# A four-layer conditioned network on one core: the steps of the conditioning are dealt out differently over its phases

## The chip, the core and the metric

The kernel runs on one core of a Trainium2 chip. Time is device time of the whole program in microseconds (us); lower is better. The engines that matter here are PE (matrix products; its weight loads are listed as PEld), DVE (elementwise work), ACT (activations), POOL (elementwise work) and SP, which here only issues transfers, one after the other. PE's clock has two levels, 1.2 and 2.4 GHz; the profile's granted clock (PEclk) is 1.00 where it ran at 2.4 GHz all the time.

## The reference, cut to what matters

Two blocks of two layers each run over 256 latent tokens and 256 context tokens of width 1024. Every layer has a mixer (gated linear attention, state space, two kinds of attention) and a feed-forward part (in the last layer, a mixture of experts). Everything is float32. Each layer's shifts, scales and gates are a product of one vector with a [1024, 6144] matrix: the **conditioning**, which is what the change moves about.

```
def first_block(x, c, ctx, c_ctx, ada_w, ada_b, ...):
    hl, hc = x, ctx
    s_lat = jax.nn.silu(c)
    s_ctx = jax.nn.silu(c_ctx)
    for i in range(DEPTH):
        m_l = jnp.split((s_lat @ ada_w[i] + ada_b[i])[:, None, :], 6, axis=-1)
        m_c = jnp.split(s_ctx @ ada_w[i] + ada_b[i], 6, axis=-1)
        ul = snake(modulate(hl, m_l[0], m_l[1]))
        uc = modulate(hc, m_c[0], m_c[1])
        ...
        hl = layer_norm(DEEPNORM_ALPHA * hl + m_l[2] * snake(yl), ln_g[i, 0], ln_b[i, 0])
        hl = layer_norm(DEEPNORM_ALPHA * hl + m_l[5] * sq_relu_mlp(modulate(hl, m_l[3], m_l[4]), ffn_w1[i], ffn_w2[i]),
                        ln_g[i, 1], ln_b[i, 1])
```

The second block has the same pattern with other norms and mixers.

## The kernel before, in words

The phases follow each other: mixer 0 (gated linear attention), feed-forward 0, mixer 1 (state space), feed-forward 1 (256 tokens only, where feed-forward 0 has 512), mixer 2 (attention), feed-forward 2 (gated, 512 tokens), mixer 3, experts. A product of float32 operands is made of three matmuls of split operands (`mm3`, L441 to L443). A unit of weights (`load`, L421) is 512 KB: SP fetches it into one of four buffers `wraw` (L431), ACT writes its upper bits to `whi` (L419), DVE the rest to `wlo` (L420). `whi` and `wlo` have four buffers each, so the loads run ahead of PE until these are full.

The conditioning (`ada`, L527) is a generator of 192 steps: 4 layers times 6 parts times 8 steps. A step fetches 512 KB of `ada_w`, and is done in one of two ways. **On PE** (L541): four products of 256 columns into the four row groups of one bank (8 records in the profile), from a buffer `araw` of a small pool of its own. **On DVE** (`on_pe` false, L559 and L562): the 512 KB go into one of the four `wraw` buffers, and DVE multiplies by the vector and adds to a sum `aacc`, once for the latents and, where the context needs the part, once more for the context; after a part's eighth step PE sums over the partitions ("pick", four products per sum). A part ends with four small DVE operations (L568 to L574); parts 2 and 5, the gates, are also written to memory, and `gates` (L624) reads them back as rows on all partitions.

Who takes steps, and when: `weave` (L591) alternates a mixer's main part with filler products, and after each main step adds a number of conditioning steps on PE (second number of `PACE`); `spread_ada` (L607) does steps on DVE after each step of a feed-forward product (`FPACE`); `project` takes one on PE per unit of weights. None goes beyond `CAPS`, which are per phase. The framework then orders each engine's instructions by when they should be ready, so that the rows on an engine are near the order of the code but not in it.

```
    def spread_ada(self, gen, a):
        for _ in gen:
            self.carry += a
            while self.carry >= 1:
                self.carry -= 1
                self.on_pe = False
                self.fill(1)
                self.on_pe = True
```

Of the kernel before, what the change touches and what calls it, by code (L numbers as in the profile page):

```python
# [13 lines left out]
PSUM = bass.MemoryType.PSUM  # L14
# [8 lines left out]
# ---------------------------------------------------------------- host layout  # L23
# [11 lines left out]
def _ws(w, n=256):  # L35
    """[K, C] -> [C/n, 128, K/128 * n]: all of K for n columns."""
    k, c = w.shape
    return _f(w.reshape(k // 128, 128, c // n, n).transpose(2, 1, 0, 3).reshape(c // n, 128, (k // 128) * n))


def _xs(w, kk=4, n=512):
    """[K, C] -> [K/(128 kk), C/n, 128, kk * n]."""
    k, c = w.shape
    return _f(w.reshape(k // (128 * kk), kk, 128, c // n, n).transpose(0, 3, 2, 1, 4)
              .reshape(k // (128 * kk), c // n, 128, kk * n))


def _xs_pad(w):
    """[K, C] with K no multiple of 512 -> [ceil(K/512), C/512, 128, 2048], k-tiles of the last unit shared out evenly."""
# [17 lines left out]
def _ev_bias(rpb):  # L67
    """Relative position bias by query and key, with the column window's -1e30: [8, 128, 2 * 256]."""
# [22 lines left out]
def _col(v):  # L91
    """[n * 128] -> [128, n]."""
    return np.asarray(v).reshape(-1, 128).T


def _ada_tiles(L, c):
    """The feature tiles of the conditioning's group c; the first layer's shift and scale come in halves."""
# [39 lines left out]
def layout(inp):  # L137
    """The arrays the program takes; every one a rearrangement of an input or a constant."""
    A = {}
# [19 lines left out]
    # GLA  # L159
# [19 lines left out]
    # SSD  # L179
# [9 lines left out]
    # second block  # L189
# [55 lines left out]
    # constants of the shapes  # L245
# [24 lines left out]
# ---------------------------------------------------------------- the program  # L270
# [11 lines left out]
# steps of filler, and of the conditioning, per step of a phase's main part  # L282
PACE = (0.7, 0.3), (0.45, 0.6), (1.3, 0.3), (1.3, 0.6), (0.9, 0.5), (0.65, 0.5), (0.25, 0.3), (1.25, 0.5), (0.26, 0.3)
# the conditioning's steps per step of the feed-forward layers, and how far it goes in each phase
FPACE = 0.35, 0, 0.25
CAPS = 72, 144, 144, 144, 144, 999, 999
# PSUM banks of the last mixer
OB = 2, 3, 1, 2
NREST = 2
# how many instructions a piece of work goes before its place, or after it  # L290
# [22 lines left out]
class Net:  # L313
# [4 lines left out]
    # ------------------------------------------------ pools, constants  # L318
    def pool(self, name, bufs=1, **k):
        """A pool and what closes it."""  # L320
# [3 lines left out]
    def banks(self, mm, tp, at=0, sc=0):  # L324
        """PSUM of a phase: accumulators, transposes, and two kinds for the mixers."""
# [62 lines left out]
    def open_h(self, es):  # L388
        """The residual, tokens on partitions: two tiles of the context, two of the latents."""
# [26 lines left out]
    # ------------------------------------------------ products of split operands  # L416
    def split(self, hi, lo, t, eng=None):
        """hi: the upper bits of t; lo: the exact rest."""
# [3 lines left out]
    def load(self, ap, n):  # L422
        """A unit of weights, split, in two halves: w(o, n) = parts of the columns o .. o + n."""
# [14 lines left out]
    def mm3(self, ps, a, b, first, last):  # L438
        """ps += a.T @ b."""
# [5 lines left out]
    def ws_acc(self, w, nm, m, x, t0, nt, ps):  # L445
        """Yields every 3072 columns or so."""
# [5 lines left out]
    def gemm_ws(self, ap, x, evac, nm=2, span=None):  # L452
        """Weights stationary: a unit of nm * 128 columns, tokens moving; evac(m, psum [columns, tokens])."""
# [8 lines left out]
    def gemm_ws_halves(self, units, x):  # L462
        """Several units at once, the context's tokens first: units = [(ap, nm, evac)]."""
# [14 lines left out]
    def gemm_xs(self, units, x, tts, n, evac, fill=0):  # L478
        """Tokens stationary: units = [(ap, ks)], each n columns of the weights of the k-tiles ks."""
# [22 lines left out]
    def unit(self, w, ks, x, pss, first, last, evac=None):  # L502
        """Part of a product with tokens stationary: pss = {token tile: psum}; w(k) the weights of k-tile k, split."""
# [8 lines left out]
    def flush(self):  # L512
        """What was put off until the tensor engine has other work behind it."""
# [10 lines left out]
    # ------------------------------------------------ conditioning  # L524
    def ada(self):
        """Every layer's conditioning vectors, in small steps."""
# [64 lines left out]
    def weave(self, main, filler, r, a=0.0):  # L591
        """After each step of main r steps of filler and a of the conditioning; then the rest of filler."""
        x = y = 0.0
        n = m = 0
        for _ in main:
# [6 lines left out]
            while y >= 1:  # L602
                y -= 1
                self.fill(1)
        k = sum(1 for _ in filler)

    def spread_ada(self, gen, a):  # L607
        """After each step of gen a of the conditioning, on the vector engine."""
# [8 lines left out]
    def need(self, L, c):  # L617
        """The conditioning's parts of layer L up to c."""
# [5 lines left out]
    def gates(self, pool, L, c, ctx=True):  # L624
        """Part c of the conditioning as rows on all partitions: {pair: [128, 1024]}."""
# [11 lines left out]
    def modvec(self, L, csh, csc, g=None, b=None):  # L637
        """Scale and shift per feature: (h*g + b) * (1 + scale) + shift."""
# [14 lines left out]
    # ------------------------------------------------ feature-major operands  # L653
    def big(self, i, h, dt=F32):
        """Half h of the 32 KB buffer i (per partition): [128, 4096]."""
# [9 lines left out]
    def fill_u(self, u, src, p, sc=None, sh=None):  # L665
        """Feature-major split copy of the token tiles src[0..1] of pair p, scaled and shifted."""
# [14 lines left out]
    def fill_u1(self, u, src, t, sc, sh):  # L681
        """The same of token tile t alone."""
# [12 lines left out]
    # ------------------------------------------------ norms  # L695
# [6 lines left out]
    def layernorm(self, t, c, pool, gb, bb, nz=3, z=None, keep=True, dump=None):  # L702
        """Called as each half c of H is there. z = (H - mean) * rstd, returned with the second half; later H = z * g + b."""
# [30 lines left out]
    def rms(self, t, c, pool, nz=4, z=None):  # L734
        """The same with H * rstd; c None: both halves at once."""
# [1563 lines left out]
```

## Time and profile before

| | |
|---|---|
| median of 3 runs (lowest, highest) | 2680.12 us (2672.77, 2683.09) |
| span of the profiled execution | 2672.4 us; the nearest run is 0.4 us above it |
| busy, share of the span | PE 94%, PEld 77%, DVE 73%, ACT 46%, POOL 25% |
| mean granted clock of PE | 0.974 |
| mixer 0 and its w_out | 0 to 418 us |
| feed-forward 0 | 418 to 795 us |
| mixer 1 and its w_out | 795 to 1212 us |
| feed-forward 1 | 1212 to 1405 us |
| mixer 2 and its w_out | 1405 to 1670 us |
| feed-forward 2 | 1670 to 2010 us |
| mixer 3, experts | 2010 to 2672 us |

PE's share is a mean over stages: some have PE at work without a gap, others have short waits of PE for DVE. What a moved step is worth is therefore read stage by stage.

### The profile page before, as it was taken

Reading aid. Unit: us, or ns where it says so; the run is one execution under the profiler, and the core shown is the slowest. Engines: PE = TensorE matmul, PEld = TensorE weight load, DVE = VectorE, ACT = ScalarE, POOL = GpSimd, SP = SyncE. Lnnn points to the kernel's source line nnn. Section 1 sums busy time; section 2 is a strip of 40 time slices with the busy share of each in tenths; the row PEclk is TensorE's granted clock in tenths of the full one; section 3 lists DMA queues with packets and bytes.
Section 4 is the critical chain, followed back from the end, with each engine's and each line's share of the span. In section 5 each row is a group of like instructions: output and inputs, shape, how many; then the busy total and the mean of one; then the engine's idle time right before and its main releaser. Section 6 shows DMA issues by size and latency. Waiting matters only on the chain.

```text
span 2672.4 us, 38317 instructions
## 1 busy us (share of the span) xinstructions
PE 2524.6 (94%) x14350; PEld 2065.7 (77%) x14350; DVE 1962.1 (73%) x3015; ACT 1239.3 (46%) x1899; POOL 659.3 (25%) x533
## 2 busy tenths in 40 slices
PE   6999999999999989899999999999999898999998
PEld 3877668877777777778988877888888676888886
DVE  3566787799988777877566457756438776999987
ACT  2433444223246555545544344322225444878775
POOL 1122334032332333424224123112124431000000
PEclk8999999999999989998999999999999998999999
DMA  8334556665642222245553225555524125999995
GB/s 283 125 129 142 195 200 205 213 219 198 209 161 94 71 67 71 71 159 173 189 188 122 78 71 174 180 194 194 191 92 163 61 72 193 341 328 356 336 334 217
DMA packets 137506, 471.66 MB, mean 176 GB/s; under 512 B 16544, under 2 KB 21792, under 8 KB 137056
## 3 DMA queue, kind: packets, MB, share of 16 engines
q1 hardware_dynamic: 131264, 458.34, 50.8%
q10 hardware_dynamic: 6048, 10.80, 1.2%
q8 instruction: 115, 1.88, 0.3%
q14 instruction: 79, 0.65, 0.1%
HBM read 467.96 MB, written 1.11 MB: 176 GB/s over the span
## 4 chain that ended last, share of the span: by engine, by line
PE 52%; DVE 8%; issue 4%; POOL 3%; ACT 2%; DMA 0%; ACTq 0%; DVEq 0%; POOLq 0%
PE b L441 15%; PE b L443 15%; PE b L442 15%; DVE wlo L420 2%; DVE FZ L1198 1%; PE b L1396 1%; POOL hrs L1371 1%; POOL Hc L1296 1%; PE b L1427 1%; PE b L1415 1%; DVE R L1269 1%; PE b L1301 1%; ACT whi L419 1%; PE b L1930 1%; PE b L2007 1%
## 5 line engine op out<-in xcount | busy, mean ns | idle before, releaser
L419 ACT ACTIVATE whi<-wraw 128x1024 fp32r<-128x1024 f32 x472 | 491.9, 1047 | 582.4 <-PE b L443 246.6
L420 DVE TENSOR_TENSOR wlo<-wraw,whi 128x1024 fp32r<-128x1024 f32 x472 | 594.4, 1268 | 209.0 <-ACT whi L419 205.4
L441 PE MATMUL b<-whi,big 128*128 128x512 f32 (+1 forms) x1696 | 600.1, 355 | 5.6 <-DVE xn L1374 4.1
L442 PE MATMUL b<-wlo,big 128*128 128x512 f32 (+1 forms) x1696 | 591.1, 349 | 5.1 <-DVE wlo L420 5.1
L443 PE MATMUL b<-whi,big 128*128 128x512 f32 (+1 forms) x1696 | 589.4, 348 | 0.6 <-POOL big L420 0.5
L441 PE MATMUL b<-big,whi 128*128 128x512 f32 (+1 forms) x1512 | 548.4, 364 | 8.4 <-ACT big L419 5.7
L443 PE MATMUL b<-big,wlo 128*128 128x512 f32 (+1 forms) x1512 | 535.9, 355 | 7.4 <-DVE wlo L420 5.5
L442 PE MATMUL b<-big,whi 128*128 128x512 f32 (+1 forms) x1512 | 535.8, 355 | 2.3 <-POOL big L420 2.1
L441 PEld LDWEIGHTS b<-whi,big 128*128 128x128 f32 x1696 | 324.3, 191 | 56.9 <-issue 13.5
L442 PEld LDWEIGHTS b<-wlo,big 128*128 128x128 f32 x1696 | 324.4, 191 | 46.5 <-DVE wlo L420 9.2
L443 PEld LDWEIGHTS b<-whi,big 128*128 128x128 f32 x1696 | 324.1, 191 | 40.5 <-issue 2.0
L441 PEld LDWEIGHTS b<-big,whi 128*128 128x128 f32 x1512 | 295.0, 195 | 55.4 <-issue 9.6
L443 PEld LDWEIGHTS b<-big,wlo 128*128 128x128 f32 x1512 | 294.6, 195 | 46.2 <-DVE wlo L420 9.0
L442 PEld LDWEIGHTS b<-big,whi 128*128 128x128 f32 x1512 | 295.0, 195 | 40.5 <-POOL big L420 5.0
L559 DVE SCALAR_TENSOR_TENSOR aacc<-wraw,s,aacc 128x1024 f32<-128x1024 f32 x161 | 232.8, 1473 | 38.3 <-DMA wraw<-in_ada 37.9
L420 POOL TENSOR_TENSOR big<-ut,big 128x256 fp32r<-128x256 f32 x101 | 105.7, 1055 | 380.9 <-ACT big L419 380.1
L420 DVE TENSOR_TENSOR wlo<-big,whi 128x1024 fp32r<-128x1024 f32 (+1 forms) x157 | 184.6, 1197 | 18.1 <-ACT whi L419 15.5
L419 ACT ACTIVATE whi<-big 128x1024 fp32r<-128x1024 f32 (+1 forms) x157 | 160.5, 1034 | 33.8 <-PE b L443 26.6
L420 POOL TENSOR_TENSOR big<-hr,big 128x512 fp32r<-128x512 f32 (+1 forms) x64 | 85.1, 1330 | 344.1 <-ACT big L419 315.4
L1198 DVE SCALAR_TENSOR_TENSOR FZ<-xp,vecs,FZ 128x512 f32<-128x512 f32 (+1 forms) x128 | 99.9, 780 | 12.8 <-ACT FZ L1196 11.7
L419 ACT ACTIVATE big<-ut 128x256 fp32r<-128x256 f32 x156 | 62.3, 412 | 84.3 <-DVE ut L676 26.9
L761 DVE TENSOR_TENSOR yt<-b,gate 128x512 f32<-128x512 f32 x92 | 63.0, 685 | 25.2 <-PE b L443 25.0
(449 smaller groups left out, 3543.2 us busy)
## 6 DMA issues: line engine op xcount, KB each, us to landing
big<-in_moe SPq DMA_DIRECT2D x148, 512.0 KB, 6.4
wraw<-in_f SPq DMA_DIRECT2D x136, 512.0 KB, 4.0
wraw<-in_ada SPq DMA_DIRECT2D x120, 512.0 KB, 4.2
araw<-in_ada SPq DMA_DIRECT2D x72, 512.0 KB, 4.1
wraw<-in_moe SPq DMA_DIRECT2D x72, 512.0 KB, 6.3
wraw<-in_g SPq DMA_DIRECT2D x68, 512.0 KB, 3.8
Hc<-in_moe SPq DMA_DIRECT2D x36, 512.0 KB, 6.8
wraw<-in_gla_o SPq DMA_DIRECT2D x16, 512.0 KB
```

The source lines that it names most:

```text
L419: self.nc.scalar.activation(hi, t, AF.Copy)
L420: (eng or self.nc.gpsimd).tensor_tensor(lo, t, hi, op=OP.subtract)
L441: mm(ps, a[0], b[0], start=first, stop=False)
L442: mm(ps, a[0], b[1], start=False, stop=False)
L443: mm(ps, a[1], b[0], start=False, stop=last)
L559: nc.vector.scalar_tensor_tensor(acc[v], raw, s, acc[v], op0=OP.mult, op1=OP.add)
L761: nc.vector.tensor_mul(y, ps, gt)
L1198: V.scalar_tensor_tensor(o, xp[:, :ns, k:k + 256], w(k), o, op0=OP.mult, op1=OP.add)
L1269: (V if t is TH else nc.gpsimd).tensor_tensor(R[z, t is TL], tri["le" if z == 0 else "ge"][:, None, :].to_broadcast([128, 4, 128]), hc(t[: ...
L1296: nc.gpsimd.tensor_tensor(ys, ys, hc4[:, 1280:1536], op=OP.add)
L1301: mm(o, ys[:, 128 * i:128 * i + 128], self.ident, start=True, stop=False)
L1371: nc.gpsimd.tensor_tensor(r, ss, self.mhalf.to_broadcast([128, nh]), op=OP.pow)
```

## The change

It changes four tables and two places of code. Comments and descriptions are dropped as well, which changes no instruction.

```
-PACE = (0.7, 0.3), (0.45, 0.6), (1.3, 0.3), (1.3, 0.6), (0.9, 0.5), (0.65, 0.5), (0.25, 0.3), (1.25, 0.5), (0.26, 0.3)
-FPACE = 0.35, 0, 0.25
-CAPS = 72, 144, 144, 144, 144, 999, 999
+PACE = (0.7, 0.18), (0.45, 0.3), (1.3, 0.3), (1.3, 0.6), (0.9, 0.5), (0.65, 0.5), (0.25, 0.3), (1.25, 0.5), (0.26, 0.3)
+FPACE = 0.32, 0.16, 0.28
+CAPS = 48, 112, 112, 128, 136, 999, 999
+ASK = 3, 3, 9
...
     def weave(self, main, filler, r, a=0.0):
...
-            while y >= 1:
-                y -= 1
-                self.fill(1)
+            if y >= 2:
+                y -= 2
+                self.fill(2)
...
-    def ffn(self, u, units1, w2, nk, gate, alpha, pairs, after, after_part, halves, pace, cap):
+    def ffn(self, u, units1, w2, nk, gate, alpha, pairs, after, after_part, halves, pace, cap, ask):
...
-            if late and n > 2:
+            if late and n >= ask:
                 gate, late = late(), None
```

Steps by phase, counted by following the generator through both programs (one vector: latents only; two: context too):

| phase | before | after |
|---|---|---|
| mixer 0, start and scans (PE) | 72 | 44, after the first 16 in twos |
| mixer 0, w_out (PE) | 0 | 4 |
| feed-forward 0 (DVE) | 72: 24 of one vector, 48 of two | 64: 32 of one, 32 of two |
| feed-forward 1 (DVE) | 0 | 16 of two |
| mixer 2 (PE) | 0 | 8, in twos |
| feed-forward 2 (DVE) | 48: 16 of two, 32 of one | 56: 24 of two, 32 of one |

In feed-forward 2 the gate rows are asked for after nine units of weights where it was three; in the other two nothing changes in that (`n > 2` and `n >= 3` are the same).

How the change lies on the engines is seen at three places. First PE, where the third scan of mixer 0 ends (L541, in the changed kernel L543: conditioning; L903 to L926, there L905 to L928: the scan's transposes, states and outputs; line numbers of the changed kernel are two higher). Before:

```order
L541 MATMUL ada<-araw,s_98 32x256
L903 MATMUL b<-ident,ek 128x128 x2
L541 MATMUL ada<-araw,s_98 32x256 x3
L926 MATMUL b<-big_134,AT 128x256
L926 MATMUL b<-S,QS 128x256
L541 MATMUL ada<-araw,s_98 32x256 x8
L926 MATMUL b<-big_134,AT 128x256
L903 MATMUL b<-ident,ek 128x128
L911 MATMUL b<-big_134,KT 128x256
```

After:

```order
L905 MATMUL b<-ident,ek 128x128
L886 MATMUL b<-big_134 64x64
L890 MATMUL b<-QS,ek 64x64 x2
L928 MATMUL b<-big_134,AT 128x256
L928 MATMUL b<-S,QS 128x256
L543 MATMUL ada<-araw,s_98 32x256 x12
L928 MATMUL b<-big_134,AT 128x256
L905 MATMUL b<-ident,ek 128x128
L913 MATMUL b<-big_134,KT 128x256
```

A step is four rows here; the three steps that stood between the transposes and the outputs now stand in one place. Next SP's queue at feed-forward 1 (`in_f_1`: its weights; `in_ada`: conditioning; gate: rows of a gate). Before, and then after, to its twelfth load of weights:

```order
L431 DMA wraw<-in_ssd_o 128x1024 x4
L431 DMA wraw<-in_f_1 128x1024 x6
L634 DMA gate_10852<-g_114 128x1024
L431 DMA wraw<-in_f_1 128x1024 x58
L431 DMA wraw<-in_ev_k 128x1024 x2
```

```order
L433 DMA wraw<-in_ssd_o 128x1024 x4
L433 DMA wraw<-in_f_1 128x1024 x2
L548 DMA wraw<-in_ada 128x1024
L433 DMA wraw<-in_f_1 128x1024 x4
L548 DMA wraw<-in_ada 128x1024
L636 DMA gate_10629<-g_114 128x1024
L433 DMA wraw<-in_f_1 128x1024 x2
L548 DMA wraw<-in_ada 128x1024
L433 DMA wraw<-in_f_1 128x1024 x4
L548 DMA wraw<-in_ada 128x1024
```

Sixteen conditioning transfers now stand between the 64 of the weights, in the same four buffers, and two more of 128 KB (biases) and four writes of 2 KB. Last, DVE in the middle of feed-forward 1 (`hr`, `yt`, `H`: the layer's own work). Before:

```order
L420 TENSOR_TENSOR wlo<-wraw,whi 128x1024 x2
L1092 TENSOR_TENSOR hr<-hr,b 128x256 x2
L420 TENSOR_TENSOR wlo<-wraw,whi 128x1024 x2
L1092 TENSOR_TENSOR hr<-hr,b 128x256
L420 TENSOR_TENSOR wlo<-wraw,whi 128x1024 x2
L761 TENSOR_TENSOR yt<-b,gate_10852 128x512
```

After:

```order
L422 TENSOR_TENSOR wlo<-wraw,whi 128x1024
L763 TENSOR_TENSOR yt<-b,gate_10629 128x512
L561 SCALAR_TENSOR_TENSOR aacc_10373<-wraw,s_101,aacc_10373 128x1024
L767 SCALAR_TENSOR_TENSOR H_3330<-H_3330,yt 128x512
L763 TENSOR_TENSOR yt<-b,gate_10629 128x512
L422 TENSOR_TENSOR wlo<-wraw,whi 128x1024
L767 SCALAR_TENSOR_TENSOR H_3331<-H_3331,yt 128x512
L422 TENSOR_TENSOR wlo<-wraw,whi 128x1024 x2
L561 SCALAR_TENSOR_TENSOR aacc_10371<-wraw,s_101,aacc_10371 128x1024
```

The sums `aacc` now stand between the weights' splits and the layer's own work. With the conditioning left out, PE's rows are the same in both programs outside the scans of mixer 0, some rows at the first units of feed-forward 1, and a few in mixer 2 and where feed-forward 2 begins; mixer 1, mixer 3 and the experts have the same rows.

## Rows read from the trace of the kernel before

**Rows 1.** The page, part 1: busy us (share of the span) xinstructions

```profile
PE 2524.6 (94%) x14350; PEld 2065.7 (77%) x14350; DVE 1962.1 (73%) x3015; ACT 1239.3 (46%) x1899; POOL 659.3 (25%) x533
```

**Rows 2.** Stretch, length, busy of PE PEld DVE ACT POOL (instructions), PEclk, DMA share, GB/s

```profile
57.00:280.00 223.00, 217.81 (x1758) 173.53 (x1758) 129.44 (x284) 88.23 (x129) 46.78 (x39) 1.00 0.43 142
280.00:358.00 78.00, 70.56 (x621) 43.44 (x620) 61.88 (x142) 32.29 (x60) 24.98 (x25) 1.00 0.54 180
358.00:418.00 60.00, 56.42 (x308) 47.73 (x308) 52.60 (x80) 26.06 (x36) 28.02 (x27) 0.97 0.63 213
460.00:580.00 120.00, 120.00 (x548) 97.10 (x548) 102.11 (x112) 32.46 (x41) 18.93 (x11) 1.00 0.66 219
580.00:740.00 160.00, 151.83 (x699) 118.86 (x698) 153.39 (x148) 41.80 (x51) 54.65 (x27) 0.98 0.62 207
1230.00:1380.00 150.00, 150.00 (x970) 137.16 (x968) 89.30 (x103) 76.46 (x113) 40.89 (x41) 1.00 0.58 192
1405.00:1610.00 205.00, 200.34 (x1319) 163.93 (x1320) 117.75 (x235) 86.73 (x175) 56.28 (x48) 1.00 0.30 95
1670.00:2010.00 340.00, 340.00 (x1582) 279.03 (x1581) 195.45 (x201) 96.86 (x117) 60.56 (x39) 1.00 0.52 171
```

**Rows 3.** The same stretches, instructions on the conditioning's bank `ada` alone: PE, PEld, DVE

```profile
57.00:280.00 223.00, 25.34 (x256) 6.08 (x256) 1.70 (x4) 1.00 0.43 142
280.00:358.00 78.00, 17.99 (x192) 4.62 (x192) 1.26 (x3) 1.00 0.54 180
```

**Rows 4.** Timeline of PE, a single step: start us, us, engine line op out<-in

```profile
168.02 0.39 PE L858 MATMUL b<-gmk,glo 128*128 128x512 f32 x1
168.34 0.64 PE L541 MATMUL ada<-araw,s 128*32 128x256 f32 x8
168.91 0.50 PE L857 MATMUL b<-gmq,ghi 128*128 128x512 f32 x1
169.25 0.39 PE L858 MATMUL b<-gmq,glo 128*128 128x512 f32 x1
169.48 0.39 PE L441 MATMUL b<-big,whi 128*128 128x512 f32 x1
```

**Rows 5.** Timeline of PE, two steps together

```profile
295.62 1.07 PE L541 MATMUL ada<-araw,s 128*32 128x256 f32 x16
297.32 0.67 PE L926 MATMUL b<-big,AT 128*128 128x256 f32 x2 [0.62 <-DVE AT L895]
```

**Rows 6.** What PE waited for from 418 to 795 us: total, times, longest

```profile
PE b L443 <- DVE wlo L420: 4.5, 2, 2.8
PE ada L541 <- DVE aacc L559: 3.2, 3, 1.2
```

**Rows 7.** Timeline of PE around the longest of these waits

```profile
648.02 0.79 PE L443 MATMUL b<-big,wlo 128*128 128x512 f32 x1 [2.83 <-DVE wlo L420]
648.61 0.63 PE L441 MATMUL b<-big,whi 128*128 128x512 f32 x1
649.03 0.63 PE L442 MATMUL b<-big,whi 128*128 128x512 f32 x1
...
653.73 0.57 PE L441 MATMUL b<-big,whi 128*128 128x512 f32 x1
654.14 0.39 PE L442 MATMUL b<-big,whi 128*128 128x512 f32 x1
```

**Rows 8.** Groups of instructions, 460 to 580 us: busy us, mean ns | idle before

```profile
L559 DVE SCALAR_TENSOR_TENSOR aacc<-wraw,s,aacc 128x1024 f32<-128x1024 f32 x39 | 56.2, 1465 | 2.7 <-DMA wraw<-in_ada 2.6
```

**Rows 9.** Groups of instructions, 1230 to 1380 us

```profile
L420 DVE TENSOR_TENSOR wlo<-wraw,whi 128x1024 fp32r<-128x1024 f32 x54 | 67.0, 1249 | 45.7 <-ACT whi L419 45.2
L419 ACT ACTIVATE whi<-wraw 128x1024 fp32r<-128x1024 f32 x53 | 55.8, 1059 | 38.7 <-PE b L443 34.7 <-PE b L442 3.8
```

**Rows 10.** What SP's queue waited for, 1230 to 1380 us

```profile
SPq L431 <- DVE wlo L420: 111.9, 40, 4.5
```

**Rows 11.** Groups of instructions over the whole span

```profile
L562 DVE TENSOR_SCALAR aacc<-wraw,s 128x1024 f32<-128x1024 f32 x23 | 21.4, 932 | 7.1 <-PE ada L541 5.3 <-DMA wraw<-in_ada 1.8
```

More of the change, by code (lines that the diff above doesn't have):

```diff
@@ L2101, in layer0 @@
         self.ffn(u, self.sqrelu_units(self.slots(pool, 0), 0, 0, 512), lambda q, c: self.A["f2_0"][q, c],
-                 [range(4 * q, 4 * q + 4) for q in range(8)], late, ALPHA, [[0, 1], [2, 3]], after, part, True, FPACE[0], CAPS[1])
+                 [range(4 * q, 4 * q + 4) for q in range(8)], late, ALPHA, [[0, 1], [2, 3]], after, part, True, FPACE[0], CAPS[1], ASK[0])
         self.ffn_es.close()
@@ L2169, in layer1 @@
         self.ffn(u, self.sqrelu_units(self.slots(pool, 1), 1, 256, 256), lambda q, c: self.A["f2_1"][q, c],
-                 [range(4 * q, 4 * q + 4) for q in range(8)], late, ALPHA, [[2, 3]], after, part, False, FPACE[1], CAPS[3])
+                 [range(4 * q, 4 * q + 4) for q in range(8)], late, ALPHA, [[2, 3]], after, part, False, FPACE[1], CAPS[3], ASK[1])
         self.ffn_es.close()
@@ L2215, in layer2 @@
         self.ffn(u, self.swiglu_units(self.slots(pool, 0)), lambda q, c: self.A["g2"][q, c], _ksplit(22),
-                 lambda: self.gates(pool, 2, 5), None, [[0, 1], [2, 3]], after, part, True, FPACE[2], CAPS[5])
+                 lambda: self.gates(pool, 2, 5), None, [[0, 1], [2, 3]], after, part, True, FPACE[2], CAPS[5], ASK[2])
         self.ffn_es.close()
```

## The prediction, as it was put on record

> **What bounds the kernel now.** I read the page's busy shares first: PE is at work for 94% of the span, the next engine, DVE, for 73% [rows 1]. So in general a microsecond of PE work costs a microsecond and one of DVE nothing; but a share over the span hides stages, so I next read the stretches [rows 2]. Four kinds are to be seen there. In the scans of mixer 0 from 57 to 280 us PE works 217.8 of 223 us at a granted clock of 1.00, DVE 129.4: PE bounds. In the last scan, 280 to 358, PE works 70.6 of 78 and DVE 61.9: PE waits here and there for DVE. In feed-forward 0 PE has no gap from 460 to 580 (120.00 of 120) with DVE at 102.1, but loses 8.2 us from 580 to 740, where DVE works 153.4 of 160. In feed-forward 1, mixer 2 and feed-forward 2 PE has no gap or nearly none, and DVE is at 60%, 57% and 57%. Third, what a conditioning step takes on PE [rows 3 to 5]; fourth, what PE waits for in feed-forward 0 [rows 6, 7]; last, in feed-forward 1, who holds the weight buffers [rows 9, 10].
>
> **The price of a step.** On PE [rows 4]: the matmul ahead starts at 168.02, the one behind the step at 168.91, 0.89 us later; without the step it would be 0.23 (169.25 to 169.48), so 0.66; and the next start comes 0.34 later where 0.23 is usual, 0.11 more. A single step costs 0.77 us; the 25.34 us on 256 records, which are 32 steps, agree (0.79 each) [rows 3]. Two steps together are busy for 1.07 us where one is for 0.64 [rows 4, 5]: the second costs 0.43, a pair 1.20. On DVE a two-vector step costs two operations of 1.465 us, but 0.93 for the first of a part [rows 8, 11]. A pick on PE is the same eight records as a step, 0.66 us where PE is not already switching.
>
> **Term by term.**
>
> Mixer 0, 57 to 280 us: 32 single steps (24.6 us) become eight pairs (9.6): 15.0 us less PE work. The bounds of what that gives are nothing, if the scan's chain over DVE sets the pace, and all of it. PE's 97.7% is nearest to all [rows 2]; the gaps between a scan's dependent products lose some cover, so I take 85%: -12.8 us.
>
> Mixer 0, 280 to 358: 24 steps (18.5 us) become 12, which stand in about seven bunches (7 x 0.77 + 5 x 0.43 = 7.5): 11.0 us less. Here PE has 7.4 us of gaps already and DVE 79% [rows 2], so the steps that leave were partly cover for waits. Bounds again nothing and all; I take 40%: -4.4 us.
>
> w_out of mixer 0: four single steps are new, 3.1 us, at PE 56.4 of 60; the 2 MB more among 213 GB/s may hold up a load, for which I add 0.7: +3.8 us. The cover of these transfers is the loads that run ahead.
>
> Feed-forward 0: 64 steps in place of 72, and 96 sums in place of 120, so 35 us less DVE work (24 x 1.465). What PE loses to DVE is 4.5 us for the weights' lower halves and 3.2 us for picks [rows 6]. After the longest of these, 2.83 us, the matmuls start 0.42 to 0.43 us apart until 653.73 and 0.23 afterwards: some 12 of them ran at 1.2 GHz, 12 x 0.20 = 2.4 us [rows 7]. Three picks fewer are 2.0 us. Together 12.1 us can go. The steps of one vector now fall in the middle of the layer, where DVE was full; at its end there are still 16 of two vectors, so some waits stay. I take two thirds: -8 us. The bounds are -2 (the picks alone) and -12.1.
>
> Feed-forward 1: 16 steps of two vectors are new. PE gets four picks, 2.6 us, and has no gap to put them in. DVE gets 4 x 0.93 + 28 x 1.465 = 44.7 us: in the 150 us from 1230, 134.0 or 89%. That lies between two rows [rows 2]: at 85% (460 to 580) PE has no gap, at 96% (580 to 740) it loses 5%. Behind each sum on DVE are queued the splits that PE needs next. And SP: before, its queue waits 111.9 of the 150 us for DVE to free one of the four `wraw` buffers [rows 10], yet nothing is late, since ACT in its turn waits 38.5 us for PE to free `whi` [rows 9]: four converted pieces lie ready. With 54 loads in 150 us [rows 9] a buffer may take 4 x 150/54 = 11.1 us per turn; with 70 transfers only 8.6 us, 2.14 us per transfer. Supply so fast is shown nowhere; 219 GB/s from 460 to 580 is 2.39 us for 524,288 bytes, but that was all that was asked for, as PE had no gap. The bounds are 2.14 (no loss) and the 2.53 us of 207 GB/s where DVE was full (70 x 2.53 - 150 = 27 us). I take 2.3, nearer to the row without a gap: 11 us over, of which the four pieces ahead cover most; 2 us stay. At the start of the layer two sums stand on DVE among the transposed features for which PE waits there: 1.5 us, one operation. Together +6 us.
>
> Mixer 2: four pairs, 4.8 us, with PE at 200.3 of 205 and transfers at 95 GB/s [rows 2]: +4.5 us.
>
> Feed-forward 2: eight steps more on DVE, 23 us, bring it from 57% to 64% beside a PE without a gap; two picks more: +1.3 us. That the gate's rows are asked for six units later costs nothing: they are first used after twelve units, and PE has no gap from 1670 on that the earlier place had made. Mixer 1, mixer 3 and the experts keep their rows and get nothing.
>
> The sum: -12.8 - 4.4 + 3.8 - 8 + 6 + 4.5 + 1.3 = -9.6 us. Made against the profiled execution that is 2672.4 - 9.6 = 2662.8 us of span. The median of the runs lies 7.7 us above that execution; against it the forecast is 2670.5 us, 0.36% less. The three runs spread over 0.4%, so a difference under 0.5% is about what a measurement of this kernel cannot tell from none.
>
> **Rivals.**
>
> All savings come whole and DVE hides all that it gets: -15.0 - 11.0 + 3.1 - 12.1 + 2.6 + 4.8 + 1.3 = -26.3, 2653.8 us. For it speaks PE's share in every stage concerned, against it the gaps of the last scan.
>
> The scans are bound by their chain, not by PE, and the steps only filled what are then waits: mixer 0 gives nothing, +3.8 for w_out stays: 3.8 - 8 + 6 + 4.5 + 1.3 = +7.6, 2687.7 us. For it speaks DVE's 79% in the last scan; against it that matmuls of 512 columns follow each other there every 0.23 us [rows 4]. The Trainium skill speaks for this rival: "Perfetto Trace Analysis", section "Identifying the Most-Contended Engine", says that PE's headroom is to be judged by the busy share of weight loads and not by that of matmuls. By it PE would have a fifth to spare in the scans, since PEld works 173.5 of 223 us. The spacing of the matmuls does not agree with it.
>
> The other side: feed-forward 1 is short of weights. If its DVE fills up and each transfer takes the 2.53 us of 580 to 740, the layer loses 27 us, and with the picks 29.6 in place of 6: -13.4 - 8 + 29.6 + 4.5 + 1.3 = +14.0, 2694.1 us. It begins at 2.14 us per transfer (a buffer held for 8.6 us) and eats up all gains (15.6 us of the other terms, less 4.1 for picks and start) at (150 + 11.5)/70 = 2.31 us, or at 2.46 us if the four pieces ahead, 11 us, are counted. For it speaks SP's waiting; against it the 120 us without a gap at 219 GB/s.
>
> DVE's sums slow down beside POOL. In 460 to 580 a sum took 1465 ns [rows 8] with POOL busy 16% of the time; if the excess over a split's 1249 ns [rows 9] grows with POOL's share (27% in feed-forward 1 [rows 2]), 216 x 27/16 = 365 ns, a sum takes 1.61 us, DVE is 5 us fuller (92%) and the layer loses some 3 us more: -6.6, 2673.5 us. Against it: a split has two inputs in the same memory too, and takes 1249 ns in feed-forward 1 with that very share of POOL. The Trainium skill has the mechanism: "SBUF — State Buffer", section "SBUF: two separate sides", says that of a DVE operation with two inputs in SBUF and a POOL operation that reads SBUF the later one stands until the earlier has finished. The trace agrees in part: sums are long, splits are not.
>
> That the tables do nothing is ruled out by the order of the rows.
>
> **How the numbers follow.** Forecast 0.46 (its own range 2661 to 2680), all savings 0.24, chain-bound scans 0.12, short of weights 0.13, slow sums 0.05. The likeliest case gives 2670.5 us. Below 2652 lies less than half of the second case, above 2691 most of the fourth, together under 0.2; that is the range. Faster by over 0.5% is below 2666.7 us: all of the second case and a quarter of the first and some of the rest's scatter, 0.37. Slower is above 2693.5 us: the larger part of the fourth and a little of the third, 0.12. Within 0.5%: 0.51.
>
> **What would show it.** In the changed kernel's stretches: mixer 0 ends its scans some 17 us earlier, with PE still near 97% in the first three; feed-forward 0 has DVE under 90% from its middle on and fewer than 3 us of waits for `wlo`; feed-forward 1 is 3 to 9 us longer, DVE near 89%, and ACT's waits for PE have turned in part into waits for transfers; mixer 2 is 4 to 5 us longer. I am wrong if PE's gaps in the scans grow by as much as its work shrinks, or if PE waits in feed-forward 1 for `wlo` by more than 10 us.

## The result, and the profile after

The changed kernel takes 2697.58 us in the median of four runs (2694.5 to 2701.48), the kernel before on the same chip 2681.61: a ratio of 1.0064, 95% interval 1.0042 to 1.0085. It is slower by 0.6%, where I had put 0.4% faster first, and the time lies above my range. The profiled execution spans 2695.9 us, 23.5 more than the 2672.4 of before.

PE's row on the page answers to [rows 1]:

```profile
PE 2515.4 (93%) x14246; PEld 2070.8 (77%) x14246; DVE 1994.2 (74%) x3039; ACT 1239.0 (46%) x1899; POOL 645.3 (24%) x533
```

PE works 9.2 us less than before and the program is 23.5 us longer, so 32.7 us of gaps were added. Where they are is seen when the span is cut at the same instruction in every kernel: the first product of a scan (L886 here), the last transposed tile of the last scan (L1019), the first `hr` of a feed-forward layer, the first `xp` of mixer 1, the last `yt` of its w_out, the last `hr` of feed-forward 1, the table load (ACT_TABLE_LOAD) with which ACT prepares the first `hr` of feed-forward 2, and the last `hr` of that layer. Lengths in us, from the first and last starts in the profiled executions; the runs e1 to e12 come below.

| | start | scans of mixer 0 | its w_out | ff 0 | mixer 1 | ff 1 | mixer 2 | ff 2 | rest |
|---|---|---|---|---|---|---|---|---|---|
| before | 101.4 | 258.8 | 59.8 | 386.9 | 395.4 | 174.8 | 291.8 | 318.4 | 685.1 |
| changed | 103.8 | 248.0 | 83.9 | 370.6 | 399.8 | 192.6 | 293.5 | 318.7 | 685.0 |
| e1 whole part | 100.0 | 244.3 | 64.9 | 369.2 | 401.0 | 189.6 | 295.0 | 318.7 | 687.2 |
| e2 bias apart | 101.8 | 247.2 | 72.9 | 368.5 | 406.4 | 190.3 | 292.8 | 318.8 | 685.2 |
| e3 ff 1 free | 97.2 | 245.5 | 86.8 | 405.7 | 395.6 | 175.0 | 291.9 | 318.8 | 684.7 |
| e4 before, split | 98.4 | 256.1 | 81.2 | 386.0 | 401.7 | 174.8 | 289.8 | 318.4 | 685.4 |
| e5 pairs alone | 100.3 | 255.3 | 59.8 | 387.2 | 398.6 | 174.9 | 289.5 | 318.4 | 686.2 |
| e6 late sums | 102.4 | 244.3 | 65.2 | 369.8 | 401.7 | 186.9 | 295.9 | 318.7 | 682.7 |
| e7 64 in scans | 100.9 | 253.8 | 61.6 | 372.4 | 402.1 | 175.1 | 291.3 | 318.7 | 684.4 |
| e8 72 in scans | 103.1 | 257.9 | 60.3 | 371.4 | 396.4 | 174.9 | 292.3 | 318.8 | 687.6 |
| e9 short sums | 102.1 | 245.8 | 65.0 | 368.7 | 401.9 | 184.4 | 295.8 | 318.8 | 686.2 |
| e10 no loads | 98.3 | 245.4 | 64.9 | 368.6 | 401.5 | 181.8 | 295.1 | 318.8 | 687.8 |
| e11 mixer 1 | 97.9 | 246.0 | 64.8 | 369.6 | 409.3 | 176.6 | 291.2 | 318.8 | 685.6 |
| e12 single | 102.1 | 256.6 | 61.6 | 372.6 | 400.1 | 174.8 | 291.7 | 318.8 | 684.2 |

A stage whose rows are untouched shows how far such a length can be trusted: mixer 1 has the same rows in before, e4 and e5 and takes 395.4, 401.7 and 398.6; the start varies by 6.6 over all runs. The scans have the same steps in e1, e6, e9, e10 and e11 and take 244.3 to 246.0, and in e5 and e8, where they take 255.3 and 257.9. Feed-forward 2 hardly varies: 318.4 with the old tables, 318.7 or 318.8 with the new ones.

The same cuts as windows of the changed kernel (columns as in [rows 2]):

```profile
103.80:351.80 248.00, 226.94 (x1863) 181.16 (x1863) 171.27 (x376) 96.21 (x160) 63.32 (x61) 0.97 0.29 99
351.80:435.70 83.90, 63.76 (x355) 52.03 (x355) 56.33 (x85) 27.56 (x38) 26.71 (x27) 0.88 0.57 200
435.70:806.30 370.60, 364.59 (x1750) 298.08 (x1749) 296.28 (x336) 124.73 (x164) 94.78 (x68) 1.00 0.60 197
1206.10:1398.70 192.60, 176.82 (x1131) 157.13 (x1132) 155.47 (x189) 89.83 (x146) 67.87 (x54) 0.95 0.64 207
```

Two stages carry the loss, w_out of mixer 0 (+24.1) and feed-forward 1 (+17.8); two give time back, the scans (-10.8) and feed-forward 0 (-16.3).

**w_out of mixer 0.** On [rows 2] PE worked 56.4 of 60 us here. Now it works 63.8 of 83.9 at a granted clock of 0.88. What PE waited for in this window:

```profile
PE b L673 <- ACT z L722: 12.6, 3, 5.5
PE b L443 <- DVE yt L763: 2.3, 1, 2.3
PE ada L543 <- DMA araw<-in_ada: 2.1, 1, 2.1
```

The transposes (L673) wait for the normed residual `z`. DVE's timeline says why that is late, and ACT's queue what DVE waits for:

```profile
358.03 1.29 DVE L763 TENSOR_TENSOR yt<-b,gate 128x512 f32<-128x512 f32 x2 [4.96 <-DMA gate<-g]
...
380.75 0.42 DVE L570 TENSOR_TENSOR aev<-ada,abias 128x256 f32<-128x256 f32 x1
...
387.92 1.29 DVE L767 SCALAR_TENSOR_TENSOR Hc<-Hc,yt 128x512 f32<-128x512 f32 x2 [4.98 <-DMA Hc<-in_x]
```

```profile
381.20 0.82 ACTq L397 DMA_DIRECT2D Hc<-in_x  x2
382.06 2.05 ACTq L397 DMA_DIRECT2D H<-in_x  x2
```

The first product of w_out is ready at 358, but the residual to which it is added is loaded only at 381.20, right behind the addition of a bias, `abias`, at 380.75. `open_h` closes the pool in which that bias lies, and gives its room to the residual. Part (0,5) of the conditioning (layer 0, part 5) was begun in the scans and ends in w_out, so its bias holds the room until its last step. In the kernel before no part was open there; the first addition to the residual came 4.8 us after the scans' end, now 36.1:

```profile
365.00 0.68 DVE L765 SCALAR_TENSOR_TENSOR Hc<-Hc,yt 128x512 f32<-128x512 f32 x1
```

**Feed-forward 1.** PE had no gap from 1230 to 1380 [rows 2]. Now the waits of PE from 1206.1 to 1398.7 are:

```profile
PE b L673 <- DVE z L751: 4.9, 1, 4.9
PE b L693 <- ACT z L722: 3.5, 1, 3.5
PE b L693 <- DVE ut L694: 3.5, 5, 1.2
PE b L445 <- DVE wlo L422: 3.1, 2, 2.6
PE b L444 <- DVE wlo L422: 2.9, 3, 1.4
```

(The waits for `ut` are not new, 5.1 us before; of the 3.5 us for ACT's `z`, 3.2 lie ahead of 1206.1.) Those of DVE in the same window, and then those of ACT from 1248 to 1398, which answer to [rows 9]:

```profile
DVE aacc L561 <- DMA wraw<-in_ada: 16.6, 6, 3.7
DVE wlo L422 <- ACT whi L421: 10.4, 13, 1.6
```

```profile
ACT whi L421 <- DMA wraw<-in_f: 42.6, 27, 4.3
...
ACT whi L421 <- PE b L445: 4.6, 3, 1.7
```

ACT waited 38.5 us for PE before; that has become 42.6 us for transfers, so the four pieces that lay ready are gone. And DVE stands 16.6 us in front of sums whose chunk has not landed, with the splits of weights behind them. The first such sum stands ahead of the third of the four `yt` of mixer 1's w_out, which comes 17.7 us behind the first where it was 15.4, so the layer's start is late too:

```profile
1198.43 1.42 DVE L564 TENSOR_SCALAR aacc<-wraw,s 128x1024 f32<-128x1024 f32 x2 [3.38 <-DMA wraw<-in_ada]
1199.76 0.75 DVE L765 SCALAR_TENSOR_TENSOR yt<-b,yrs,gate 128x512 f32<-128x512 f32 x1
```

**Feed-forward 0** is without a gap also where it lost 8.2 us before [rows 2], with DVE at 80%; the waits of [rows 6] for `wlo` and `aacc` are gone from the view:

```profile
476.00:596.00 120.00, 120.00 (x559) 96.59 (x558) 95.89 (x108) 35.88 (x44) 18.76 (x13) 1.00 0.67 222
596.00:756.00 160.00, 160.00 (x733) 129.21 (x732) 127.55 (x133) 48.22 (x57) 41.89 (x27) 1.00 0.62 202
```

### The profile page after: what moved, and what is told of

It is laid out like the page before. It is cut to its first block, busy times and chain, and to the rows that moved or that the text cites. A ratio compares the mean times of both kernels' runs of the same rounds, so it can differ in the third digit from the quotient of the medians.

```text
span 2695.9 us, 38139 instructions
## 1 busy us (share of the span) xinstructions
PE 2515.4 (93%) x14246; PEld 2070.8 (77%) x14246; DVE 1994.2 (74%) x3039; ACT 1239.0 (46%) x1899; POOL 645.3 (24%) x533
## 4 chain that ended last, share of the span: by engine, by line
PE 49%; DVE 10%; POOL 3%; issue 3%; DMA 2%; ACT 2%; ACTq 0%; DVEq 0%; POOLq 0%; SPq 0%
PE b L443 14%; PE b L445 13%; PE b L444 13%; DVE wlo L422 3%; DMA wraw<-in_ada 1%; DVE FZ L1200 1%; PE b L1398 1%; POOL hrs L1373 1%; POOL Hc L1298 1%; ACT whi L421 1%; PE b L1429 1%; PE b L1303 1%; DVE R L1271 1%; PE b L1417 1%; PE b L1306 1%
## 5 line engine op out<-in xcount | busy, mean ns | idle before, releaser
L445 PEld LDWEIGHTS b<-big,wlo 128*128 128x128 f32 x1512 | 295.0, 195 | 43.4 <-DVE wlo L422 6.4
L444 PEld LDWEIGHTS b<-big,whi 128*128 128x128 f32 x1512 | 295.9, 196 | 39.7 <-POOL big L422 4.2
L561 DVE SCALAR_TENSOR_TENSOR aacc<-wraw,s,aacc 128x1024 f32<-128x1024 f32 x182 | 258.5, 1445 | 53.5 <-DMA wraw<-in_ada 53.2
L1200 DVE SCALAR_TENSOR_TENSOR FZ<-xp,vecs,FZ 128x512 f32<-128x512 f32 (+1 forms) x128 | 99.1, 774 | 12.1 <-ACT FZ L1198 10.9
L700 POOL TENSOR_TENSOR rstd<-ve,mhalf 128x1 f32<-128x1 f32 x42 | 32.0, 762 | 225.8 <-DVE ve L717 101.5
```

Of the source, the lines that this page charges most:

```text
L444: mm(ps, a[0], b[1], start=False, stop=False)
L445: mm(ps, a[1], b[0], start=False, stop=last)
L561: nc.vector.scalar_tensor_tensor(acc[v], raw, s, acc[v], op0=OP.mult, op1=OP.add)
L700: self.nc.gpsimd.tensor_tensor(r, ve, self.mhalf.to_broadcast([128, ve.shape[1]]), op=OP.pow)
L1200: V.scalar_tensor_tensor(o, xp[:, :ns, k:k + 256], w(k), o, op0=OP.mult, op1=OP.add)
```

## Experiments

**e1 and e2: the late residual, or the steps in w_out.** e1 ends the part in the scans, e2 leaves all steps where they are and moves one allocation.

```
# e1
-PACE = (0.7, 0.18), (0.45, 0.3), ...
+PACE = (0.7, 0.18), (0.45, 0.44), ...
# e2
-bias = self.ar.tile([128, 256], F32, name="abias", bufs=1)
+bias = self.tmp.tile([128, 256], F32, name="abias", bufs=1)
```

> The changed kernel, with the last scan of mixer 0 taking 14 steps of the conditioning in place of 10, so that part (0,5) is finished in it and no step stands in w_out. Theory A (part (0,5) lies across the change of rooms, the residual's loads wait until its bias has been read, and the residual is late): the first hr of feed-forward 0 comes at 418 to 423 us in place of 435.7, the whole is 12 to 18 us shorter than the changed kernel, 2680 to 2686 us, no slower than the kernel before by more than 0.3%. Rival B (the four steps with their transfers among the weights of w_out cost it, wherever the residual lies): the same here; the next run tells them apart. Rival C (the loss comes from the scans, whose gaps lost their cover, and w_out only inherits it): two pairs more in the last scan, hr at 436 to 438 us, 2698 to 2700 us.

> The changed kernel with one allocation moved: the bias of a conditioning part lies in the pool of scratch tiles and no longer in the pool that is closed when the residual is opened. All steps stay where they are, four of them in w_out. Theory A: the residual's loads are issued near 355 us in place of 381.2, the first addition to it comes near 365 in place of 387.9, hr at 418 to 424 us, the whole 12 to 18 us shorter than the changed kernel. Rival B (the steps' own price): the loads come early, but hr stays at 432 to 436 us and the whole within 3 us of the changed kernel. Rival C: as B.

e1: 2672.19 us, 0.9987 of before (0.9973 to 1.0001); e2: 2682.1 us, 1.0017 (1.0002 to 1.0031). From the changed kernel's median that is 25 and 15 us, or 21 and 13 by the ratios, as the kernel before was itself some 4 us faster in that series. w_out falls from 83.9 to 72.9 us by the allocation alone, and to 64.9 without the steps. So theory A holds for the first 11 us, and B for another 8: more than the 12 to 18 us forecast for e1, because both are true. (The cut moves a little: in e1 and e2 20 matmuls of 256 columns more than in the changed kernel, the first of feed-forward 0, start ahead of its first `hr`. Taken together with that layer, e2 is 13.1 us below the changed kernel and e1 another 7.3.) In e2 the residual comes 7.2 us behind the scans' end, ahead of the bias:

```profile
355.04 1.29 DVE L763 TENSOR_TENSOR yt<-b,gate 128x512 f32<-128x512 f32 x2 [4.78 <-DMA gate<-g]
356.25 1.28 DVE L767 SCALAR_TENSOR_TENSOR Hc<-Hc,yt 128x512 f32<-128x512 f32 x2
...
386.68 0.41 DVE L570 TENSOR_TENSOR aev<-ada,abias 128x256 f32<-128x256 f32 x1
```

What the four steps still cost in e2 is shown by SP's queue (a row's second number is the time from its first issue to its last) and by PE:

```profile
348.05 20.22 SPq L548 DMA_DIRECT2D araw<-in_ada  x4
368.36 8.07 SPq L433 DMA_DIRECT2D wraw<-in_gla_o  x5
```

```profile
360.26 1.08 PE L543 MATMUL ada<-araw,s 128*32 128x256 f32 x8 [4.18 <-DMA araw<-in_ada]
```

Four chunks for two `araw` buffers stand in the queue ahead of five loads of w_out's weights, which are issued 20 us later; PE waits 4.2 us for the first, and its work of 3.1 us comes on top: 7.3 of the 8. In the changed kernel the chunks stand otherwise, between the loads, and PE waited 2.1 us for one of them, so how its own 24.1 us divide between bias and chunks is not shown exactly:

```profile
350.85 1.50 SPq L548 DMA_DIRECT2D araw<-in_ada  x2
360.48 0.33 SPq L433 DMA_DIRECT2D wraw<-in_gla_o  x1
361.72 0.33 SPq L548 DMA_DIRECT2D araw<-in_ada  x1
362.14 0.94 SPq L433 DMA_DIRECT2D wraw<-in_gla_o  x2
```

Rival C is out: more pairs in the last scan (e1) made it no longer.

**e4: the split part alone, in the kernel before.**

```
-PACE = (0.7, 0.3), (0.45, 0.6), ...
+PACE = (0.7, 0.3), (0.45, 0.42), ...
```

> The kernel before, with the last scan of mixer 0 taking 16 steps in place of 20, so that the last four of a part, (1,2), fall into w_out; single steps, and every other table as before. Theory A: the residual's loads wait for the part's bias as in the changed kernel; hr of feed-forward 0 comes 10 to 18 us later than 420.0, the whole 8 to 18 us slower than before. Rival B (four steps among w_out's weights cost little more than their work, 3.1 us, which the scan saves): within 3 us of before. Rival C: 1 to 3 us faster or slower, since only a scan's cover changes.

2693.62 us, 1.0069 (1.0052 to 1.0086). One number, by which a part is left open at `open_h`, costs w_out 21.4 us (81.2 against 59.8), with the same sign in the trace:

```profile
383.83 0.42 DVE L568 TENSOR_TENSOR aev<-ada,abias 128x256 f32<-128x256 f32 x1
...
389.79 1.29 DVE L765 SCALAR_TENSOR_TENSOR Hc<-Hc,yt 128x512 f32<-128x512 f32 x2 [3.77 <-DMA Hc<-in_x]
```

By its ratio it is as large as the whole change's loss. Theory A holds; B and C do not come near.

**e3: feed-forward 1 without steps.**

```
-FPACE = 0.32, 0.16, 0.28
-CAPS = 48, 112, 112, 128, 136, 999, 999
+FPACE = 0.42, 0, 0.28
+CAPS = 48, 128, 128, 128, 136, 999, 999
```

> The changed kernel with the 16 steps of feed-forward 1 done in feed-forward 0 (80 steps there in place of 64, 128 sums in place of 96). Theory D (the sums on DVE make feed-forward 1 late: one that waits for its transfer ahead of the residual at its start, the late second rms, the weights' lower halves later): from the end of mixer 1 to mixer 2 the layer is 16 to 18 us shorter, with less than 1 us of waits for wlo and none of 4.85 us for z; feed-forward 0 becomes 8 to 16 us longer, like before; the whole 0 to 10 us shorter than the changed kernel. Rival E (feed-forward 1 lost its time to the clock and to the order of rows, not to the sums): the layer keeps at least 8 us of its loss, and the whole is slower than the changed kernel by 2 to 10 us.

2711.9 us, 1.0145 (1.0121 to 1.0168): slower still. The layer itself did what theory D says, 175.0 us in place of 192.6, so all of its loss hangs on the 16 steps. But feed-forward 0 paid 35.1 us for them, where I had put 8 to 16, and the forecast of the total is wrong. By sums on DVE that layer takes 371.4 us for 88 (e8), 368.5 to 372.6 for 96, 386.0 to 387.2 for 120, 405.7 for 128: flat, then steep. PE's waits there come back (429.5 to 835.2 us of e3):

```profile
PE b L444 <- DVE wlo L422: 6.9, 3, 3.8
PE ada L543 <- DVE aacc L561: 6.2, 2, 4.0
```

**e6, e9 and e10: what in feed-forward 1 costs.** All three start from e1, whose layer takes 189.6 us. e6 starts the steps with the sixth unit; e9 shortens the sums; e10 leaves out their transfers.

```
# e6 (with 0.2 in FPACE for this layer)
-self.spread_ada(self.gemm_ws(ap, u, ev, span=lambda _: (t0, nt)), pace)
+self.spread_ada(self.gemm_ws(ap, u, ev, span=lambda _: (t0, nt)), pace if halves or n >= 5 else 0)
# e9, for the parts (2,2) and (2,3)
+o = slice(0, 64) if ff1 else slice(0, 1024)
+nc.vector.scalar_tensor_tensor(acc[v][:, o], raw[:, o], s, acc[v][:, o], op0=OP.mult, op1=OP.add)
# e10, for the same parts
+if L == 2 and c in (2, 3) and not pe:
+    raw = self.fpool.tile([128, 1024], F32, name="kept", bufs=1) if k == 0 else last
...
+if L == 2 and c in (2, 3) and not pe and k:
+    pass
+else:
     nc.sync.dma_start(raw, self.A[f"ada{b}"][i, c, k])
```

> The changed kernel with the whole part of run e1 (no step in w_out of mixer 0), and in feed-forward 1 the 16 steps start with the sixth unit of weights in place of the first, so behind the residual, the transposes and the second rms; all 16 stay in the layer. From the last product of mixer 1's residual to the last hr of feed-forward 1: 174.8 us in the kernel before, 192.6 in the changed one, 189.6 in the run with a whole part. Theory D1 (the seam at the layer's start is half of the loss: a sum that waits for its transfer ahead of the residual, a late second rms, PE at half its clock behind that): 179 to 183 us, with 5 to 9 us of waits for wlo left, the whole 7 to 10 us faster than the run with a whole part. Rival D2 (DVE's load over the layer is all of it, wherever the sums stand): 187 to 192 us, no difference to that run. Rival D3 (16 sums' worth in fewer units crowd the splits): above 192 us, waits for wlo above 12 us.

> The run with a whole part, but in feed-forward 1 each sum behind the first of a part takes 64 of its 1,024 columns (28 sums; the conditioning of these two parts is then not computed); all 16 transfers, the picks and the rows stay. From mixer 1's last yt to the layer's last hr: 174.8 us before, 189.6 in the run with a whole part. Theory J (DVE's time for the sums is what delays the splits): 176 to 180 us, only the picks (2.6) and a little of the start remain. Rival K (the 16 transfers crowd the weights: they take buffers and bandwidth): 185 to 190 us, no difference. Between the two, 181 to 184, both count.

> The run with a whole part, but in feed-forward 1 each part loads its first chunk of the conditioning only, into a tile of its own, and sums that chunk eight times: 14 of 16 transfers and all weight buffers of the conditioning are left out (the conditioning of these two parts is then not computed), all 32 sums and the picks stay. Same stretch. Theory J (DVE's time): 186 to 190 us. Rival K (transfers and buffers): 176 to 180 us. Both: between.

e6: 2670.36 us, 0.9976 (0.9963 to 0.999); e9: 2667.58, 0.9958 (0.9943 to 0.9973); e10: 2667.43, 0.9968 (0.9955 to 0.998). The layer takes 186.9, 184.4 and 181.8 us. So neither single theory holds. Late sums take the waits for `z` at the start away, 4.9 and 2.9 us in e1, but the layer gives back all but 2.7: the same sums stand closer, and the waits for `wlo` are 6.3 us against 5.5. That is nearest to D2. Short sums give 5.2 us, no transfers 7.8, and the waits for `wlo` (5.5 us in e1) fall to 0.8 and 0.3. What remains in both are the picks and, above all, the start of the layer: in e9 PE still waits 4.6 us for `z`, and of the 9.6 us that its layer is longer than before, 7.0 have been lost at the twelfth of its 32 `hr`. In e9 DVE has time, yet stands longer in front of its sums; in e10 that wait is gone:

```profile
DVE aacc L563 <- DMA wraw<-in_ada: 26.0, 11, 3.8
```

So behind the start it takes both to make PE wait for `wlo`: with short sums DVE's longer waits for chunks cost PE 0.8 us there, and long sums without those waits 0.3. Nor is the rate of the transfers the limit: in e9, with all 16 chunks, PE has 0.9 us of gaps in the layer's last 131 us, at 235 GB/s:

```profile
1237.00:1367.90 130.90, 130.01 (x822) 115.33 (x821) 84.11 (x115) 61.83 (x90) 31.61 (x30) 1.00 0.71 235
```

(In e10, 7 of the 28 long sums fall ahead of the stretch, which makes its 181.8 a little too good.)

**e5 and e12: the pairs by themselves.** e5 puts the pairs alone into the kernel before, e12 takes them out of e7.

```
# e5; e12 is the reverse
-while y >= 1:
-    y -= 1
-    self.fill(1)
+if y >= 2:
+    y -= 2
+    self.fill(2)
```

> The kernel before with one edit: the chunks of the conditioning on PE are taken by twos. 72 single steps in mixer 0 (0.77 us each, 55.4 us) become 36 pairs (1.20 us each, 43.2 us), 12.2 us less PE work in the scans; tables as before. From the first product of a scan to the last transposed tile (258.8 us in the kernel before, 248.0 in the changed one, 244.3 in the run with a whole part). Theory F (the scans are bound partly by PE and partly by their chain over DVE, so about half of the PE work that leaves comes back as time): 252 to 254 us, the whole 5 to 7 us faster than before. Rival G (PE sets the pace there): 246 to 248 us, the whole 11 to 13 us faster. Rival H (the chain sets it): 257 to 260 us, no difference.

> The run with 64 steps in the scans, with the chunks on PE taken singly again (64 single steps in mixer 0 in place of 32 pairs, 8 in mixer 2 in place of 4); every other number as there. Theory F2 (taking them by twos alone is worth little in these scans: 3.5 us were measured for 36 pairs, where the step prices give 12.2): scans 254 to 258 us against 253.8, the whole within 4 us of the run with 64 steps. Rival G (the pairs carry that run's gain, 32 x 0.34 = 10.9 us): scans 262 to 266 us, the whole 10 to 13 us slower than that run.

e5: 2673.22 us, 0.999 (0.9975 to 1.0006), no difference; scans 255.3 us against 258.8, between what F and H gave. e12: 2665.7 us, 0.9954 (0.9939 to 0.9969), 4.8 us above e7 in the median (F2 had up to 4), with overlapping intervals; its scans are 2.8 us longer, as F2 has it, and hardly more than the 2.6 by which e5 and e8 differ. The windows of the scans of e7, then e12:

```profile
100.90:354.70 253.80, 235.65 (x2008) 181.94 (x2007) 168.91 (x392) 96.28 (x160) 66.94 (x61) 0.99 0.39 135
```

```profile
102.10:358.70 256.60, 243.58 (x2007) 180.09 (x2007) 170.11 (x392) 96.25 (x160) 66.06 (x61) 0.99 0.40 134
```

Pairs take 7.9 us of work off PE, and 5.1 of them come back as gaps.

**e7, e8 and e11: other tables, from what was found.** Whole parts at `open_h`, nothing in feed-forward 1, about 96 sums in feed-forward 0.

```
# e7
+PACE = (0.7, 0.3), (0.45, 0.42), ...   FPACE = 0.32, 0, 0.28   CAPS = 64, 128, 128, 128, 136, ...
# e8
+PACE = (0.7, 0.3), (0.45, 0.6), ...    FPACE = 0.28, 0, 0.28   CAPS = 72, 128, 128, 128, 136, ...
# e11
+PACE = (0.7, 0.18), (0.45, 0.44), ...  FPACE = 0.32, 0, 0.28   CAPS = 48, 112, 128, 128, 136, ...
```

> Pairs as in the changed kernel, but other tables: 64 steps in the scans of mixer 0 (ended there, no part left over), 64 in feed-forward 0, none in mixer 1 and feed-forward 1, 8 in mixer 2, the rest as in the changed kernel. If the three causes are right (late residual and steps in w_out; sums in feed-forward 1; scans whose PE work counts half), it has the scans at 246 to 251 us, w_out at 60 to 66, feed-forward 0 at 368 to 372, feed-forward 1 at 174 to 176, and is 2655 to 2663 us, 0.5 to 0.8% faster than before. If the steps' work in the scans counts whole (16 more than in the changed kernel, 8 pairs, 9.6 us), 2664 to 2670 us.

> As the run with 64 steps in the scans, but 72 there (36 pairs) and 56 in feed-forward 0, with 88 sums on DVE in place of 96. If feed-forward 0 still gains from fewer sums (16.3 us for 24 sums from before to the changed kernel, 0.68 each), it is 3 to 6 us shorter there, 364 to 367 us, for 1 to 5 us more in the scans: within 4 us of that run. If PE is full in feed-forward 0 already (98.8% in the changed kernel), only the picks count: 369 to 371, and the whole 1 to 5 us slower than that run.

> The run with a whole part, with the 16 steps of feed-forward 1 done as eight pairs in mixer 1 (four scans, two pairs each), where PE works 88 to 91% of the time and no step stood. Feed-forward 1 as before the change, 174 to 176 us (189.6 in the run with a whole part). If a step in mixer 1 costs its PE work, 8 x 1.20 = 9.6 us, the whole is some 5 us faster than the run with a whole part, 2666 to 2669 us; if mixer 1's chain hides it, 2655 to 2660 us; if it delays that chain, as sums and steps did elsewhere, 2672 us or more.

e7: 2660.92 us, 0.9934 (0.9908 to 0.9959); e8: 2664.53, 0.9953 (0.9937 to 0.9969); e11: 2661.2, 0.9933 (0.9908 to 0.9959). All beat both kernels. In e7 the scans went past the forecast (253.8 against 246 to 251): 16 steps more than in e1 cost 9.5 us, their whole price of 9.6. In e8 feed-forward 0 gained 1.0 us from eight sums fewer, and the scans paid 4.1 (1.5 by e5, whose scans are the same as e8's). In e11 feed-forward 1 takes 176.6 us, near the 174.8 of before, and mixer 1 took 409.3 us, 8.3 above e1: near the steps' price of 9.6, but only 2.9 above e2, which has no step there, so the size is not settled.

## Why the prediction was wrong

| term | forecast | measured |
|---|---|---|
| scans of mixer 0 | -12.8 - 4.4 | -10.8 (-14.5 in e1) |
| w_out of mixer 0 | +3.8 | +24.1 |
| feed-forward 0 | -8 | -16.3 |
| feed-forward 1 | +6 | +17.8 |
| mixer 2 | +4.5 | +1.7 |
| feed-forward 2 | +1.3 | +0.3 |
| start, mixer 1, rest | 0 | +6.7 |
| sum | -9.6 | +23.5 |

The line before the sum, 2.4 us of the start and 4.4 of mixer 1, is within the scatter of these stages.

**w_out of mixer 0 is the step that failed.** I priced the four steps by their work and 0.7 us for a load, with "the loads that run ahead" as their cover. Two things were missing: that the bias of an unfinished part holds the residual's room (11 us, e2; in the kernel before the split alone costs 21.4, e4), and that the steps' chunks stand among w_out's weights in SP's queue (8 us with their work, e1 against e2). Some 5 us of the 24.1 stay in e1, where PE works 60.2 us in this stretch against 56.2: 31 matmuls of feed-forward 0 more stand in it, which is work moved and not lost. Both causes could be read beforehand: 44 steps at the end of the scans are no multiple of eight, and `open_h` closes the pool.

**Feed-forward 1: right in kind, mis-sized.** It cost +17.8 in place of +6, all of it due to the 16 steps (e3); the terms that were too small are the 2 us left over behind the pieces ahead and the 1.5 us at the layer's start. I let the four pieces ahead cover most of 11 us; they were used up, as ACT's waits show. The 2.3 us per transfer was right (229 GB/s from 1248 to 1398, 2.29 us for 524,288 bytes); the 2.53 us of the rival "short of weights" did not come, and neither did the 10 us of waits for `wlo` that I had named as a sign: 6.0. That this rival's total, 2694.1, lies near the measured 2697.6 is luck, since it has w_out at +3.8. What I had not counted is that a sum waiting for its chunk holds the splits behind it (16.6 us of such waits). The layer's start, put at 1.5 us, cost more: 4.9 us for `z` and, behind that wait, PE at a granted clock of 0.89, so partly at 1.2 GHz, from 1230 to 1260. At the twelfth of the layer's 32 `hr` 7.1 of the 17.8 us had been lost.

**The scans: about half right.** Steps that leave do give time; joining steps hardly does (3.5 us in e5, 2.8 in e12, near the scatter). PE's work there fell by 22.0 us from before to e1 and the scans by 14.5:

```profile
101.40:360.20 258.80, 246.42 (x2072) 179.87 (x2072) 172.47 (x396) 96.53 (x160) 65.33 (x61) 1.00 0.46 152
100.00:344.30 244.30, 224.43 (x1894) 177.85 (x1894) 169.79 (x380) 96.30 (x160) 64.25 (x61) 0.99 0.32 109
```

My single saving of 15.0 and 11.0 us did not part the two. The rival that the chain sets the pace is wrong for fewer steps and nearly right for pairs. The rule of the Trainium skill beside it ("Perfetto Trace Analysis", section "Identifying the Most-Contended Engine") looked at PEld, at work 180 of 258.8 us; PEld's work stayed at 178 in e1 while the time fell by 14.5 us, so it did not tell the pace here.

**Feed-forward 0: right in kind, twice as large.** My upper bound was 12.1. The waits for `wlo` and for sums went entirely, as e3 shows from the other side. PE's gaps fell by 8.2 us (14.3 to 6.0), close to the 7.7 of [rows 6]; the term that was too small is PE's work, which fell by 8.0 (372.6 to 364.6) where I had 2.0 for picks and 2.4 for the clock. 11 matmuls that now start ahead of the cut are a part of that.

**Mixer 2 and feed-forward 2.** Mixer 2 was priced at nearly all of its new work, 4.5 us; 1.7 is within its scatter (289.5 to 291.8 without the steps). Feed-forward 2 was right: the table load at which it is cut stands elsewhere in the changed kernel, and from its first `hr` to its last (1673.0 to 1987.3 before, 1695.4 to 2010.9 now) the layer takes 1.2 us more, where I had 1.3.

**Slow sums beside POOL** did not come: in feed-forward 1 POOL is busy 35% of the time and a sum takes 1381 ns, less than the 1465 of [rows 8]. So the rule of "SBUF — State Buffer" (the Trainium skill, section "SBUF: two separate sides"), by which a DVE operation with two inputs in SBUF and a POOL operation that reads SBUF wait for each other, gave these sums no price here that grows with POOL's share:

```profile
L561 DVE SCALAR_TENSOR_TENSOR aacc<-wraw,s,aacc 128x1024 f32<-128x1024 f32 x28 | 38.3, 1381 | 16.6 <-DMA wraw<-in_ada 16.6
```

## What to carry to other kernels

Before work is spread by a table of numbers, look where a group that it cuts holds something, a tile or a place in an in-order queue, that other work needs: its price is then not its work. A layer whose bound engine has no gap still lives on what lies ready ahead of it; count how much of that is used up, and, on an engine with little time to spare, put no instruction that waits for a transfer ahead of those that feed the bound engine. Price an edit of the schedule in gaps as well as in work: of the 7.9 us of work that pairs saved (e7 against e12) some two thirds came back as gaps.

## What the runs showed that was not expected

A stage with the same rows varied by 6 us between executions (mixer 1: 395.4, 401.7, 398.6). Splits of weights in feed-forward 1, 1249 ns before [rows 9], took 1343 ns in the changed kernel's 1248 to 1398 us; why, no run here settles:

```profile
L422 DVE TENSOR_TENSOR wlo<-wraw,whi 128x1024 fp32r<-128x1024 f32 x52 | 69.0, 1343 | 10.8 <-ACT whi L421 9.5 <-PE b L444 1.2
```
